# MLP start of a diffusion-backbone kernel: four direct tiles with the last modulation, then seven-product pairs, and the sums of h2 made during the four tiles

## The chip, the core and the metric

The kernel runs on one core of a Trainium2 chip. A core has a matrix engine (PE, 128x128, with its weight loads shown as PEld), a vector engine (DVE), a scalar engine (ACT), GpSimd (POOL) and a sync engine (SP); SP and POOL issue the DMAs. Each engine works through its own queue in order and waits on semaphores. The metric is the device time of one execution in microseconds (us), median of the runs. Before the change it is 1055.24 us (three runs, 1054.97 to 1055.71).

## The reference

One inference step of a layer over 128 context tokens and 512 latent tokens of width 1024. The first sub-layer mixes tokens, the second is a squared-ReLU MLP:

```
mod = silu(c) @ w_ada + b_ada                    # six rows of 1024
h   = layer_norm(x) * (1 + mod[1]) + mod[0]
tm, sf, sb = token_mixer(h, ...)                 # S5 scan, pooling, gates
x   = layer_norm(ALPHA * x + mod[2] * tm) * ln1_g + ln1_b
h2  = layer_norm(x) * (1 + mod[4]) + mod[3]
f   = square(relu(h2 @ w_mlp1 + b_mlp1)) @ w_mlp2 + b_mlp2
x   = layer_norm(ALPHA * x + mod[5] * f) * ln2_g + ln2_b
```

All is float32. The change touches the line of f and the modulation mod[5], the gate of its residual.

## The kernel before

All 640 tokens are handled together, as five token tiles of 128. A float32 operand is split into a high part, rounded to the format that PE reads (a cast on ACT, L321), and the low rest (a subtraction on DVE, L322). A product is three passes: high by high, high by low, low by high. `wsplit` loads one 128x1024 weight block by SP into one of two raw buffers and splits it.

The MLP has 32 hidden tiles of 128 in four quarters of eight. A quarter's first product makes eight tiles f from h2 (`fx`), the second multiplies them with w_mlp2 into two halves of the output, 120 matmuls of 512 columns each, and adds gate times result to x (`add_gated`, L851 and L852). In quarters 2 to 4 two hidden tiles are made together, by seven half-size products in place of eight (`mlp_pair`; Strassen's scheme in Winograd's form). That needs sums of the four blocks of h2 (t1, t2, t4, and t3 in the place of the block b12), made once by `rhs_sums`, and sums of the weights' blocks for each pair (s12, s34, split into w12 and w34; `lhs_pair`). A pair takes 84 matmuls of 320 columns; an ordinary tile 24 of 384 columns and 24 of 256, since h2 is cut after 384 tokens.

The first quarter is different. Its tiles 0 to 4 are made together (`mlp_first`), first for 384 tokens, then for the other 256, so that PE has work while the last token tile of h2 is still in the norm. Tiles 5 to 7 follow one by one (`mlp_in`). Between them stand eight steps of the last modulation (`ada5.step`: four matmuls with a 128x1024 weight loaded by POOL; the class `Ada`, L236), and then `gates`: the finished row gets its bias (L778), is written to DRAM and read back by SP as two tiles with the row in every partition (L783). `rhs_sums` is a generator: one of its eight parts is recorded with each weight of the second product. `residual` (L1045, L1046: x times ALPHA plus bias times gate, for five token tiles) is recorded with the second weight.

A scheduler of the tile framework sets the order on each engine and puts the semaphores; pools with a fixed number of slots decide when a tile can be written: nine slots `x4` (five hold x), eight slots `h` (the out projection's inputs `mx`, later `fx`), three `w10`, two raw weight buffers.

Of the kernel before, what the change touches and what calls it, by code (L numbers as in the profile page):

```python
# [11 lines left out]
F32R = mybir.dt.float32r  # L12
# [5 lines left out]
P = 128  # L18
D = 1024
# [12 lines left out]
SEG_MLP = ((0, 384), (384, 256))  # L32
# [6 lines left out]
def hybrid_kernel(ctx: ExitStack, tc: tile.TileContext, xin, cc, w_ada0, w_ada, w_in, w_glu, w_pa, w_pool, w_pb,  # L39
# [35 lines left out]
    def bank(name="ax"):  # L75
        return pp[0].tile([P, 512], F32, tag="ax", bufs=axn[0], name=nm(name))
# [197 lines left out]
    wa_h = lambda: hslot([P, D], F32, "wa")  # L274
# [49 lines left out]
    def wsplit(src, n=D, to=None):  # L324
        raw = wp.tile([P, D], F32, tag="wr", bufs=2, name=nm("wr"))
        hl = wp.tile([P, 2, D], F32R, tag="wh", name=nm("wh")) if to is None else to
        dma(raw[:, 0:n], src)
        split(raw[:, 0:n], hl[:, 0, 0:n], hl[:, 1, 0:n])
        return hl
# [9 lines left out]
    def mm(hl, xk, segs=SEG):  # L339
        ps = bank2()  # L340
        for k in range(len(xk)):
            mm_k(ps, hl, xk[k], k, len(xk), segs)
        return ps
# [34 lines left out]
    for k in range(KT):  # L378
        pa, pb = bank("pst"), bank("pst")
# [376 lines left out]
    def w8(shape, dtype, name):  # L756
        return xp.tile(shape, dtype, tag="w8", name=nm(name))
# [6 lines left out]
    def brow_tile(src, tile_of, name="brow"):  # L764
        t = tile_of([P, D], name)
        dma(t, src.broadcast_to([P, D]))
        return t
# [6 lines left out]
    def gates(ada, i):  # L774

        row, br = row_tile(), x4([P, 256], "br")
        dma(br, rows[ada.mod].rearrange("(q f) -> q f", q=4).unsqueeze(1).broadcast_to([4, 32, 256]))
        V.tensor_tensor(row, ada.ps[:, 0:256], br, op=ALU.add)  # L778
        dma(grd[i], row)
        gs = []  # L780
        for r in range(2):
            g = xp.tile([P, D], F32, tag="gate", bufs=2, name=nm("gate"))
            dma(g.rearrange("p (q f) -> p q f", q=4),  # L783
                grd[i].rearrange("(q r) f -> r q f", q=4)[r:r + 1].broadcast_to([P, 4, 256]))
            gs.append(g)
        return gs
# [123 lines left out]

    h2k = [h2[:, :, k, :] for k in range(KT)]

    def mlp_in(m):
        ps = mm(wsplit(w_m1[m]), h2k, SEG_MLP)
        return mlp_act(m, [ps[:, n, 0:ln] for n, (_, ln) in enumerate(SEG_MLP)])

    def mlp_act(m, pss):
        fr = x4([P, NT], "fr")
        for (o, ln), ps in zip(SEG_MLP, pss):
            S.activation(fr[:, o:o + ln], ps, AF.Relu, bias=colt[:, C_BM1 + m:C_BM1 + m + 1])  # L920
        V.tensor_tensor(fr, fr, fr, op=ALU.mult)
        f = hslot([P, 2, NT], F32R, "fx")
        split(fr, f[:, 0, :], f[:, 1, :])
        return f

    def mlp_first():

        hls = [wsplit(w_m1[m], to=None if m < 3 else w8([P, 2, D], F32R, "wm")) for m in range(5)]
        pa, pb, pc_ = bank2(), bank2(), bank2()
        x0, x1 = bank("psx"), bank("psx")  # L930
        pss = [[pa[:, 0], pa[:, 1], pb[:, 0], pb[:, 1], pc_[:, 0]],
               [pc_[:, 1], pc_[:, 1, 256:512], x0, x0[:, 256:512], x1]]
        for n, (o, ln) in enumerate(SEG_MLP):
            for hl, ps in zip(hls, pss[n]):
                for k in range(KT):
                    for i, (wh, xh) in enumerate(PASS):
                        T.matmul(ps[:, 0:ln], hl[:, wh, k * P:(k + 1) * P], h2k[k][:, xh, o:o + ln],
                                 start=(k == 0 and i == 0), stop=(k == KT - 1 and i == 2))
        return [mlp_act(m, [pss[n][m][:, 0:ln] for n, (_, ln) in enumerate(SEG_MLP)]) for m in range(5)]

# [3 lines left out]
    def rhs_sums():  # L946
        b11, b12, b21, b22 = [h2[:, :, 4 * i:4 * i + 4, j * HN:(j + 1) * HN] for i in range(2) for j in range(2)]
        t1, t2, t4 = [w10("t").rearrange("p a (k c) -> p a k c", k=4) for _ in range(3)]
        rq.update(b11=b11, b21=b21, b22=b22, t1=t1, t2=t2, t3=b12, t4=t4)

        def whole(b, k):
            f = x4([P, 2, HN], "bf")
            V.tensor_tensor(f, b[:, 0, k:k + 2].bitcast(F32), b[:, 1, k:k + 2].bitcast(F32), op=ALU.add)
            return f

        def put(t, k, f):
            split(f, t[:, 0, k:k + 2], t[:, 1, k:k + 2])

        for k in (0, 2):
            f12, f11 = whole(b12, k), whole(b11, k)  # L960
            V.tensor_tensor(f11, f12, f11, op=ALU.subtract)
            put(t1, k, f11)
            yield
            f22 = whole(b22, k)
            V.tensor_tensor(f12, f22, f12, op=ALU.subtract)
            put(b12, k, f12)
            yield
            V.tensor_tensor(f22, f22, f11, op=ALU.subtract)
            put(t2, k, f22)
            yield  # L970
            f21 = whole(b21, k)
            V.tensor_tensor(f21, f21, f22, op=ALU.subtract)
            put(t4, k, f21)
            yield

    def lhs_pair(m):

# [64 lines left out]
    def residual():  # L1042
        for t in range(NTT):
            tmp = x4([P, D], "tmp")
            V.tensor_tensor(tmp, b2, g5[0 if t else 1], op=ALU.mult)  # L1045
            V.scalar_tensor_tensor(x1s[t], x1s[t], ALPHA, tmp, op0=ALU.mult, op1=ALU.add)  # L1046

    for qf in range(3):
        if qf == 0:
            ada5.load(2)  # L1050
            fx = mlp_first()
            for i, n in ((5, 3), (6, 3), (7, 2)):
                ada5.step(n)
                if i == 7:
                    g5 = gates(ada5, 1)
                    b2 = brow_tile(brow[3:4, :], x4)
                fx.append(mlp_in(i))
        else:
            fx = mlp_in8(qf * 8)
        sums = rhs_sums() if qf == 0 else iter(())  # L1060
        for fh in range(2):
            pa, pb, pc_ = bank2(), bank2(), bank("ps4")
            pt = [pa[:, 0], pa[:, 1], pb[:, 0], pb[:, 1], pc_]
            for kp in range(4):
                hl = wsplit(w_m2[fh, qf * 4 + kp])
                next(sums, None)
                if qf + fh == 0 and kp == 1:
                    residual()
                for kk in range(2):
                    k = 2 * kp + kk  # L1070
                    for t in range(NTT):
                        for i, (wh, xh) in enumerate(PASS):
                            T.matmul(pt[t], fx[k][:, xh, t * P:(t + 1) * P], hl[:, wh, kk * 512:(kk + 1) * 512],  # L1073
                                     start=(k == 0 and i == 0), stop=(k == 7 and i == 2))
            for t in range(NTT):
                add_gated(x1s[t], g5[0 if t else 1], pt[t], fh * 512, fh * 512 + 512)
# [119 lines left out]
```

## Time and profile before

| what | value |
|---|---|
| median of three runs | 1055.24 us |
| profiled execution | 1057.73 us, of which the span is 1056.0 us |
| PE, DVE, ACT, POOL busy | 94%, 65%, 38%, 11% of the span |
| mean granted clock of PE | 0.98 |
| first quarter of the MLP | about 607 to 734 us of the span |

The profile is of one execution. A timeline row gives the start, the length, the engine, the source line, the operation, output<-inputs with their shapes, the count, and in brackets the idle time before it with what ended it. Equal instructions that follow each other are merged into a row. Rows of SP (SPq) and POOL for DMAs show the issue, not the transfer. The granted clock is a share of 2.4 GHz.

### The profile page before, as it was taken

Reading aid. Unit: us, or ns where it says so; the run is one execution under the profiler, and the core shown is the slowest. Engines: PE = TensorE matmul, PEld = TensorE weight load, DVE = VectorE, ACT = ScalarE, POOL = GpSimd, SP = SyncE. Lnnn points to the kernel's source line nnn. Section 1 sums busy time; section 2 is a strip of 40 time slices with the busy share of each in tenths; the row PEclk is TensorE's granted clock in tenths of the full one; section 3 lists DMA queues with packets and bytes.
Section 4 is the critical chain, followed back from the end, with each engine's and each line's share of the span. In section 5 each row is a group of like instructions: output and inputs, shape, how many; then the busy total and the mean of one; then the engine's idle time right before and its main releaser. Section 6 shows DMA issues by size and latency. Waiting matters only on the chain.

```text
span 1056.0 us, 18416 instructions
## 1 busy us (share of the span) xinstructions
PE 991.3 (94%) x7464; PEld 894.4 (85%) x7464; DVE 691.6 (65%) x1203; ACT 403.0 (38%) x683; POOL 110.9 (11%) x164
## 2 busy tenths in 40 slices
PE   4998989998998899999999999989999999999997
PEld 2887878988897799998987898868998899889886
DVE  7698769998921334545847955498864586458686
ACT  5457454322212534422222544313661266116610
POOL 0243210310069000300000000000000000000000
PEclk9999899999999798999999999999999999999999
DMA  9566666855498587977752134513222222212421
GB/s 362 191 176 179 168 182 194 255 166 170 119 284 248 161 253 244 360 231 252 247 182 83 31 110 155 150 45 100 81 100 73 68 80 100 80 60 81 162 78 60
DMA packets 117373, 166.85 MB, mean 158 GB/s; under 512 B 48104, under 2 KB 80872, under 8 KB 117288
## 3 DMA queue, kind: packets, MB, share of 16 engines
q1 hardware_dynamic: 111912, 146.27, 43.9%
q0 software_dynamic: 5376, 19.40, 5.4%
q8 instruction: 59, 0.97, 0.4%
q14 instruction: 26, 0.21, 0.1%
HBM read 135.30 MB, written 30.34 MB: 157 GB/s over the span
## 4 chain that ended last, share of the span: by engine, by line
PE 61%; DVE 16%; DMA 10%; issue 6%; ACT 5%; SPq 2%; DVEq 0%; ACTq 0%; POOL 0%; POOLq 0%
PE ps L336 20%; PE ps L1073 13%; PE ps L1006 8%; PE psx L1006 6%; PE pse L1096 3%; PE ps L886 3%; DVE wh L322 2%; DMA cf<-in_cpk_dram 2%; DMA yd<-y 2%; DVE ta L501 1%; DVE zt L504 1%; PE psa L236 1%; PE psz L480 1%; DVE ta L503 1%; PE ps L1096 1%
## 5 line engine op out<-in xcount | busy, mean ns | idle before, releaser
L336 PE MATMUL ps<-hk,wh 128*128 128x320 f32 x1344 | 217.1, 318 | 10.0 <-DVE sq L542 5.1
L336 PEld LDWEIGHTS ps<-hk,wh 128*128 128x128 f32 x1344 | 202.0, 192 | 18.6 <-issue 6.0
L322 DVE TENSOR_TENSOR wh<-wr,wh 128x1024 fp32r<-128x1024 f32 (+1 forms) x113 | 128.5, 1138 | 101.8 <-ACT wh L321 100.7
L321 ACT CAST wh<-wr 128x1024 fp32r<-128x1024 f32 (+1 forms) x113 | 109.3, 967 | 164.7 <-PE ps L1073 87.6
L1073 PE MATMUL ps<-wh,fx 128*128 128x512 f32 x720 | 166.1, 392 | 5.2 <-DVE x L852 3.0
L1073 PEld LDWEIGHTS ps<-wh,fx 128*128 128x128 f32 x720 | 135.7, 189 | 34.2 <-DVE x L852 3.4
L336 PEld LDWEIGHTS ps<-gx,wh 128*128 128x128 f32 x384 | 56.4, 187 | 3.3 <-issue 2.9
L336 PE MATMUL ps<-gx,wh 128*128 128x320 f32 x384 | 58.7, 310 | 0.0
L336 PEld LDWEIGHTS ps<-vx,wh 128*128 128x128 f32 x384 | 56.4, 188 | 2.5 <-ACT sg L813 2.1
L336 PE MATMUL ps<-vx,wh 128*128 128x320 f32 x384 | 58.1, 311 | 0.0
L224 POOL DMA_DIRECT2D wa<-in_w_ada_dram x32 | 16.9, 534 | 300.8 <-PE psa L236 110.2
L1006 PE MATMUL psx<-h,wh 128*128 128x320 f32 x288 | 47.5, 308 | 0.0
L1006 PE MATMUL ps<-h,w 128*128 128x320 f32 x288 | 46.5, 307 | 0.0
L438 POOL TENSOR_TENSOR cf<-cf 128x64 f32<-128x64 f32 x32 | 24.8, 776 | 191.0 <-DMA cf<-in_cpk_dram 95.7
L1006 PEld LDWEIGHTS psx<-h,wh 128*128 128x128 f32 x288 | 43.7, 187 | 0.2
L1006 PEld LDWEIGHTS ps<-h,w 128*128 128x128 f32 x288 | 43.2, 187 | 0.0
L573 PE MATMUL psy<-zt,q 64*128 64x80 f32 x512 | 42.1, 276 | 0.6 <-issue 0.6
L851 DVE TENSOR_TENSOR ps<-ps,gate 128x512 f32<-128x512 f32 (+2 forms) x39 | 28.1, 749 | 19.2 <-PE ps L1073 14.2
L573 PEld LDWEIGHTS psy<-zt,q 64*128 64x128 f32 x512 | 35.3, 190 | 4.2 <-issue 4.2
L886 PE MATMUL ps<-wo,mx 128*128 128x512 f32 x150 | 36.6, 392 | 0.7 <-ACT wo L321 0.7
L336 PE MATMUL ps<-ybx,wh 128*128 128x320 f32 x192 | 32.6, 328 | 2.7 <-ACT wh L321 2.7
L886 PEld LDWEIGHTS ps<-wo,mx 128*128 128x128 f32 x150 | 27.9, 188 | 7.2 <-ACT wo L321 1.5
(263 smaller groups left out, 1656.9 us busy)
## 6 DMA issues: line engine op xcount, KB each, us to landing
wr<-in_w_m_dram SPq DMA_DIRECT2D x64, 512.0 KB
wa<-in_w_ada_dram POOLq DMA_DIRECT2D x32, 512.0 KB, 5.0
wr<-in_w_in_dram SPq DMA_DIRECT2D x28, 512.0 KB
qd<-q SPq DMA_DIRECT2D x16, 512.0 KB
q<-qd SPq DMA_DIRECT2D x16, 512.0 KB
x<-in_xin_dram SPq DMA_DIRECT2D x10, 512.0 KB
wa<-in_w_ada_dram SPq DMA_DIRECT2D x10, 512.0 KB
tm<-sd SPq DMA_DIRECT2D x8, 512.0 KB
```

Of the source, the lines that this page charges most:

```text
L224: nc.gpsimd.dma_start(w, w_ada[self.mod, :, k * D:(k + 1) * D])
L236: T.matmul(self.ps[32 * q:32 * q + 32, 0:256], sc[:, k, :], w[:, q * 256:(q + 1) * 256], start=(k == 0), stop=(k == KT - 1), skip_group_ch ...
L321: S.copy(hi, raw)
L322: V.tensor_tensor(lo, raw, hi.bitcast(F32), op=ALU.subtract)
L336: T.matmul(ps[:, n, 0:ln], hl[:, wh, k * P:(k + 1) * P], xk[:, xh, o:o + ln], start=(k == 0 and i == 0), stop=(k == nk - 1 and i == 2))
L438: E.tensor_tensor(c[:, :, 3, :], c[:, :, 1, :], c[:, :, 2, :], op=ALU.add)
L573: T.matmul(o, q[d, l, i, :], zt[d, 0:NC // 2, i, 4 * e + l, :], start=(i == 0), stop=False, skip_group_check=True)
L851: V.tensor_tensor(ps, ps, g[:, c0:c1], op=ALU.mult)
L886: T.matmul(ps[:, n, :], mx[k][:, xh, t * P:(t + 1) * P], wo[k][:, wh, n * 512:(n + 1) * 512], start=(k == 0 and i == 0), stop=(k == KT - 1 ...
L1006: T.matmul(ps, hl[:, wh, c + k * P:c + (k + 1) * P], rq[b][:, xh, k, :], start=(start and k == 0 and i == 0), stop=(stop and k == 3 and i ...
L1073: T.matmul(pt[t], fx[k][:, xh, t * P:(t + 1) * P], hl[:, wh, kk * 512:(kk + 1) * 512], start=(k == 0 and i == 0), stop=(k == 7 and i == 2))
L1096: T.matmul(ps[n][:, 0:ln], fx[k][:, xh, t * P:(t + 1) * P], hl[:, wh, o_:o_ + ln], start=(k == 0 and i == 0), stop=(k == 7 and i == 2))
```

## The change

Only four tiles are made by `mlp_first`; tiles 4 to 7 become two pairs. All eight weights of the last modulation are loaded ahead, into `h` slots (`wa_h`), and its eight steps stand in the four tiles' loop, one behind each tile of each part. `rhs_sums` is an ordinary function now, called when the 384-token part is recorded; only the writing of t3, which overwrites a block of h2, is left to the end of the four tiles. `gates` and the residual's bias come before pair 4, `residual` between pair 4 and pair 6.

```
-    def mlp_in(m):
-        ps = mm(wsplit(w_m1[m]), h2k, SEG_MLP)
-        return mlp_act(m, [ps[:, n, 0:ln] for n, (_, ln) in enumerate(SEG_MLP)])
...
-        hls = [wsplit(w_m1[m], to=None if m < 3 else w8([P, 2, D], F32R, "wm")) for m in range(5)]
+        hls = [wsplit(w_m1[m], to=None if m < 3 else w8([P, 2, D], F32R, "wm")) for m in range(4)]
         pa, pb, pc_ = bank2(), bank2(), bank2()
-        x0, x1 = bank("psx"), bank("psx")
-        pss = [[pa[:, 0], pa[:, 1], pb[:, 0], pb[:, 1], pc_[:, 0]],
-               [pc_[:, 1], pc_[:, 1, 256:512], x0, x0[:, 256:512], x1]]
+        pss = [[pa[:, 0], pa[:, 1], pb[:, 0], pb[:, 1]],
+               [pc_[:, 0], pc_[:, 0, 256:512], pc_[:, 1], pc_[:, 1, 256:512]]]
         for n, (o, ln) in enumerate(SEG_MLP):
             for hl, ps in zip(hls, pss[n]):
...
-        return [mlp_act(m, [pss[n][m][:, 0:ln] for n, (_, ln) in enumerate(SEG_MLP)]) for m in range(5)]
+                ada5.step(1)
+            if n == 0:
+                last_sums = rhs_sums()
+        fx = [mlp_act(m, [pss[n][m][:, 0:ln] for n, (_, ln) in enumerate(SEG_MLP)]) for m in range(4)]
+        last_sums()
+        return fx
...
             put(t1, k, f11)
-            yield
             f22 = whole(b22, k)
             V.tensor_tensor(f12, f22, f12, op=ALU.subtract)
-            put(b12, k, f12)
-            yield
+            late.append((k, f12))
...
+        return lambda: [put(b12, k, f) for k, f in late]
...
         if qf == 0:
-            ada5.load(2)
+            ada5.tile_of = wa_h
+            ada5.load(8)
             fx = mlp_first()
-            for i, n in ((5, 3), (6, 3), (7, 2)):
-                ada5.step(n)
-                if i == 7:
-                    g5 = gates(ada5, 1)
-                    b2 = brow_tile(brow[3:4, :], x4)
-                fx.append(mlp_in(i))
+            g5 = gates(ada5, 1)
+            b2 = brow_tile(brow[3:4, :], x4)
+            fx += mlp_pair(4)
+            residual()
+            fx += mlp_pair(6)
...
                 hl = wsplit(w_m2[fh, qf * 4 + kp])
-                next(sums, None)
-                if qf + fh == 0 and kp == 1:
-                    residual()
```

On PE, the end of the direct tiles stood before as follows (psx is the last tiles' sum, psa the modulation's row, ps_7021 tile 5):

```order
L937 MATMUL psx_6724<-h_6177,wm_6711 128x256 x24
L937 MATMUL psx_6725<-h_6177,wm_6716 128x256 x24
L236 MATMUL psa_7001<-wa_6692,sc 32x256 x4
L236 MATMUL psa_7001<-wa_6694,sc 32x256 x4
L336 MATMUL ps_7021<-h_6177,wh_7017 128x384
```

Now pair 4 follows the fourth tile (wh_7042 and w_965, w_966 are its weights, w_965 being w12; the h of wh_7185 is pair 6's, t_6845 and t_6844 are sums of h2):

```order
L933 MATMUL ps_6730<-h_6177,wm_6723 128x256 x24
L236 MATMUL psa_6755<-wa_6706,sc 32x256 x4
L1005 MATMUL psx_7060<-h_6177,wh_7042 128x320 x19
L1005 MATMUL psx_7061<-t_6845,w_965_7049 128x320 x2
L1005 MATMUL ps_7062<-t_6844,w_965_7049 128x320 x2
L1005 MATMUL psx_7061<-t_6845,w_965_7049 128x320 x10
L1005 MATMUL ps_7062<-t_6844,w_965_7049 128x320 x10
L1005 MATMUL ps_7062<-h_6177,w_966_7054 128x320 x12
L1005 MATMUL psx_7060<-h_6177,wh_7042 128x320 x5
L1005 MATMUL psx_7203<-h_6177,wh_7185 128x320 x4
L1005 MATMUL ps_7062<-h_6177,w_966_7054 128x320 x12
```

The three tiles that followed, with the steps between them, are replaced by two pairs, and the second matmul group of pair 4 reads sums of h2 and w12.

On DVE, the first pair's weight sums (s) and w12 stood before in the second product of the first quarter, behind the last sums of h2 (bf, t):

```order
L322 TENSOR_TENSOR t_7249<-bf_7481,t_7249 128x640
L972 TENSOR_TENSOR bf_7559<-bf_7559,bf_7481 128x640
L322 TENSOR_TENSOR wh_7608<-wr_7604,wh_7608 128x1024
L322 TENSOR_TENSOR t_7250<-bf_7559,t_7250 128x640
L987 TENSOR_TENSOR s_1011_7611<-wr_7606 128x512
L991 TENSOR_TENSOR s_1012_7612<-wr_7604,wr_7606 128x512
L988 TENSOR_TENSOR s_1011_7611<-s_1011_7611,wr_7604 128x512
L992 TENSOR_TENSOR s_1012_7612<-wr_7604,s_1011_7611 128x512
L322 TENSOR_TENSOR w_1013_7615<-s_1011_7611,w_1013_7615 128x1024
```

Now they stand behind the sums, the activations of the four tiles (fr, fx) and the modulation's row:

```order
L917 TENSOR_TENSOR fr_7009<-fr_7009 128x640
L917 TENSOR_TENSOR fr_7016<-fr_7016 128x640
L322 TENSOR_TENSOR fx_7006<-fr_7002,fx_7006 128x640
L322 TENSOR_TENSOR fx_7013<-fr_7009,fx_7013 128x640
L322 TENSOR_TENSOR fx_7020<-fr_7016,fx_7020 128x640
L778 TENSOR_TENSOR row_7027<-psa_6755,br_7028 128x256
L986 TENSOR_TENSOR s_963_7045<-wr_7040 128x512
L990 TENSOR_TENSOR s_964_7046<-wr_7038,wr_7040 128x512
L987 TENSOR_TENSOR s_963_7045<-s_963_7045,wr_7038 128x512
L991 TENSOR_TENSOR s_964_7046<-wr_7038,s_963_7045 128x512
L322 TENSOR_TENSOR w_965_7049<-s_963_7045,w_965_7049 128x1024
L322 TENSOR_TENSOR w_966_7054<-s_964_7046,w_966_7054 128x1024
```

From the last token tile's first split to w_965 DVE now has 32 operations of 128x640.

On DVE, the residual (tmp, x) stood before among the second product's weights and evacuations:

```order
L322 TENSOR_TENSOR wh_7382<-wr_7381,wh_7382 128x1024
L322 TENSOR_TENSOR h_6177<-bf_7251,h_6177 128x2x320
L1045 TENSOR_TENSOR tmp_7298<-brow_7177,gate_7175 128x1024
L1045 TENSOR_TENSOR tmp_7301<-brow_7177,gate_7173 128x1024
L1046 SCALAR_TENSOR_TENSOR x_777_5598<-x_777_5598,tmp_7298 128x1024
```

Now it stands among pair 4's additions (L1016 to L1028) and in front of pair 6's sums; the additions free the sums that pair 4's last products go into:

```order
L322 TENSOR_TENSOR wh_7185<-wr_7181,wh_7185 128x1024
L1016 TENSOR_TENSOR fr_7064<-psx_7061,fr_7064 128x320
L1019 TENSOR_TENSOR fr_7064<-ps_7062,fr_7064 128x320
L1020 TENSOR_TENSOR fr_7064<-ps_7062,fr_7064 128x320
L1044 TENSOR_TENSOR tmp_7166<-brow_7036,gate_7034 128x1024
L322 TENSOR_TENSOR wh_7200<-wr_7183,wh_7200 128x512
L1045 SCALAR_TENSOR_TENSOR x_777_5598<-x_777_5598,tmp_7166 128x1024
L1025 TENSOR_TENSOR fr_7063<-ps_7062,fr_7064 128x320
L1044 TENSOR_TENSOR tmp_7169<-brow_7036,gate_7032 128x1024
L1045 SCALAR_TENSOR_TENSOR x_778_5600<-x_778_5600,tmp_7169 128x1024
L1028 TENSOR_TENSOR fr_7064<-ps_7062,fr_7064 128x320
```

The first use of a gate is now in front of L1025 and of everything of pair 6 but its first weight.

## Rows read from the trace of the kernel before

**Rows 1.** The page: engines' busy time, share of the span, instructions.
```profile
PE 991.3 (94%) x7464; PEld 894.4 (85%) x7464; DVE 691.6 (65%) x1203; ACT 403.0 (38%) x683; POOL 110.9 (11%) x164
```
**Rows 2.** Stages: length, busy PE, PEld, DVE, ACT, POOL (instructions), clock, DMA, GB/s.
```profile
645.80:672.00 26.20, 25.85 (x196) 22.14 (x193) 9.12 (x11) 6.10 (x10) 3.14 (x6) 1.00 0.56 190
672.00:700.00 28.00, 27.92 (x124) 22.81 (x122) 20.46 (x21) 7.72 (x10) 0.00 (x0) 1.00 0.30 76
700.00:708.00 8.00, 2.83 (x12) 2.03 (x12) 8.00 (x13) 1.78 (x2) 0.00 (x0) 0.97 0.18 66
734.00:784.00 50.00, 50.00 (x337) 49.18 (x336) 39.35 (x58) 28.49 (x42) 0.00 (x0) 1.00 0.22 76
```
**Rows 3.** Waits of PE, 590 to 740: total us, times, longest.
```profile
PE ps L1073 <- DVE wh L322: 2.2, 1, 2.2
```
**Rows 4.** Timeline of PE, first quarter of the MLP.
```profile
607.09 5.02 PE L937 MATMUL ps<-h,wh 128*128 128x384 f32 x28
...
639.07 5.81 PE L937 MATMUL psx<-h,wm 128*128 128x256 f32 x48
...
657.95 0.64 PE L236 MATMUL psa<-wa,sc 128*32 128x256 f32 x8
...
672.10 27.82 PE L1073 MATMUL ps<-wh,fx 128*128 128x512 f32 x122
...
707.96 25.91 PE L1073 MATMUL ps<-wh,fx 128*128 128x512 f32 x107 [3.00 <-DVE x L852]
```
**Rows 5.** Timeline, end of the out projection and last token tile's norm.
```profile
600.29 6.96 PE L886 MATMUL ps<-wo,mx 128*128 128x512 f32 x30
...
606.29 1.05 ACT L321 CAST wh<-wr 128x1024 fp32r<-128x1024 f32 x1 [4.47 <-DMA wr<-in_w_m_dram]
...
619.84 1.21 DVE L322 TENSOR_TENSOR wm<-wr,wm 128x1024 fp32r<-128x1024 f32 x1
...
625.82 0.69 DVE L322 TENSOR_TENSOR h<-h2f,h 128x512 fp32r<-128x512 f32 x1 [3.21 <-ACT h L321]
```
**Rows 6.** DMA, 432 to 456: queue's share of 16 engines; issues, KB, us to landing.
```profile
q0 software_dynamic: 2086, 7.56, 79.9%
...
wa<-in_w_ada_dram POOLq DMA_DIRECT2D x9, 512.0 KB, 11.0
```
**Rows 7.** The page: DMA issues of the whole span, KB, median us to landing.
```profile
wa<-in_w_ada_dram POOLq DMA_DIRECT2D x32, 512.0 KB, 5.0
```
**Rows 8.** DVE by line and shape, 600 to 760: busy us, mean ns.
```profile
L322 DVE TENSOR_TENSOR wh<-wr,wh 128x1024 fp32r<-128x1024 f32 x17 | 20.7, 1218 | 7.4 <-ACT wh L321 7.2
...
L953 DVE TENSOR_TENSOR bf<-h 128x640 f32<-128x640 f32 x8 | 6.5, 822 | 0.0
...
L1045 DVE TENSOR_TENSOR tmp<-brow,gate 128x1024 f32<-128x1024 f32 x5 | 5.9, 1220 | 5.9 <-issue 5.9
...
L987 DVE TENSOR_TENSOR s<-wr 128x512 f32<-128x512 f32 x3 | 2.0, 683 | 0.0
```
**Rows 9.** Timeline of DVE, two sums' operations one behind the other.
```profile
716.15 0.83 DVE L953 TENSOR_TENSOR bf<-h 128x640 f32<-128x640 f32 x1
...
716.89 0.83 DVE L968 TENSOR_TENSOR bf<-bf,bf 128x640 f32<-128x640 f32 x1
```
**Rows 10.** Timeline, from the modulation's row to the first use of a gate.
```profile
670.22 0.33 SPq L779 DMA_DIRECT2D grd<-row  x1
...
672.53 0.93 SPq L783 DMA_DIRECT2D gate<-grd  x2
...
688.06 2.36 DVE L1045 TENSOR_TENSOR tmp<-brow,gate 128x1024 f32<-128x1024 f32 x2 [5.91 <-issue]
...
689.31 1.06 ACT L321 CAST wh<-wr 128x1024 fp32r<-128x1024 f32 x1 [7.89 <-DMA wr<-in_w_m_dram]
```
**Rows 11.** Timeline of PE, restart after a wait.
```profile
346.73 0.90 PE L336 MATMUL ps<-ph,wh 128*128 128x320 f32 x2 [7.87 <-ACT ph L321]
```
**Rows 12.** Stage behind that restart, columns as in rows 2.
```profile
346.70:355.00 8.30, 8.27 (x37) 7.32 (x38) 3.06 (x6) 2.47 (x4) 0.00 (x0) 0.50 0.27 93
```

More of the change, by code (lines that the diff above doesn't have):

```diff
@@ L957, in put @@
             split(f, t[:, 0, k:k + 2], t[:, 1, k:k + 2])
+        late = []
         for k in (0, 2):
@@ L962, in rhs_sums @@
             put(t1, k, f11)
-            yield
             f22 = whole(b22, k)
             V.tensor_tensor(f12, f22, f12, op=ALU.subtract)
-            put(b12, k, f12)
-            yield
+            late.append((k, f12))
             V.tensor_tensor(f22, f22, f11, op=ALU.subtract)
             put(t2, k, f22)
-            yield
             f21 = whole(b21, k)
@@ L973, in rhs_sums @@
             put(t4, k, f21)
-            yield
+        return lambda: [put(b12, k, f) for k, f in late]
     def lhs_pair(m):
@@ L1049, in hybrid_kernel @@
         if qf == 0:
-            ada5.load(2)
+            ada5.tile_of = wa_h
+            ada5.load(8)
             fx = mlp_first()
-            for i, n in ((5, 3), (6, 3), (7, 2)):
-                ada5.step(n)
-                if i == 7:
-                    g5 = gates(ada5, 1)
-                    b2 = brow_tile(brow[3:4, :], x4)
-                fx.append(mlp_in(i))
+            g5 = gates(ada5, 1)
[3 more added lines that the diff above has]
+            fx += mlp_pair(6)
         else:
             fx = mlp_in8(qf * 8)
-        sums = rhs_sums() if qf == 0 else iter(())
         for fh in range(2):
```

## Prediction

> **What bounds the kernel now.** I read the page first: the matrix engine (PE) is busy for 94% of the span [rows 1], so time is lost only where PE waits or runs on a slow clock. The change lies in the first quarter of the MLP, so I next read the stages of that quarter, one by one. While tiles 5 to 7 run (645.8 to 672.0) the vector engine (DVE) has 9 us of work in 26; in the first half of the second product it has 20 in 28, and between 700 and 708 it is busy all the time while PE does 2.8 us of work [rows 2]. The reader is to see that DVE is idle beside the first product and crowded beside the second. The waits of PE in this quarter are short: 2.2 us for a weight's low half that stands behind other DVE work, and 3.0 us for the sums into x [rows 3, 4]. So before the change at most some 5 us of waiting can be won here, and the quarter ends, for this argument, where the last matmul of its second product ends: 707.96 + 25.91 = 733.9 us [rows 4].
>
> **What goes on PE.** From the starts and lengths of runs of equal matmuls, one with 384 columns takes 5.02/28 = 0.179 us, with 256 columns 5.81/48 = 0.121; the second product's take 27.82/122 = 0.228 [rows 4]. The second quarter's four pairs, 336 matmuls with 320 columns, fill 734 to 784: 50/337 = 0.148 [rows 2]. Four direct tiles cost 4 x 24 x (0.179 + 0.121) = 28.8 us; two pairs cost 2 x 84 x 0.148 = 24.9. PE saves 3.9 us of work. The eight modulation steps stay eight, 0.6 us each (0.64 by the row, less the overlap with the next) [rows 4]. Their loads now go into the slots of the out projection's inputs, each as soon as the last token tile has read it, so they are in place before PE wants them; the wait they had cost is a few tenths.
>
> **The start of the vector chain.** The last token tile's matmuls, 0.232 us each (6.96/30), end at 607.25 [rows 5]; each six of them free one slot, 1.4 us, so the eight loads of 512 KB are issued between 597 and 607, beside the third and fourth MLP weight's. Before, the third weight's cast began at 606.29 after a wait of 4.47 for its load [rows 5]. How much that load is slowed isn't shown. From 432 to 456, among nine such loads that filled 79.9% of the engines, they took 11.0 us to land [rows 6] where 5.0 is the usual [rows 7]: 2.2 times as long. Bounds: 0, and 1.2 times the wait, 5.4. I take 2.2 us, nearer to 0, since the eight come spread over ten microseconds. ACT holds the norm's square root behind that cast, and the last token tile's norm hangs on it, so PE, too, is 2.2 late. The Trainium skill, page "DMA: Bandwidth & Descriptors", section "Queues, rings and completion order", says that each DMA engine takes turns between queue rows packet by packet. By that rule a weight's load beside the eight keeps half of each engine and is late by no more than it takes alone, 4.5 us: as an estimate, by the rule the sum below would be at most 30.8, by the row's 2.2 times at most 31.7. No row of before shows which of the two holds.
>
> The first half of the last token tile's split started at 625.82 and takes 0.69; the split of a fifth weight in front of it, 1.2 us, is gone [rows 5]. So DVE can begin the sums at 626.5 - 1.2 + 2.2 = 627.5.
>
> **The sums before the first pair.** By the order, between that point and the low half of w12, which the first pair's second multiplication needs, DVE now has 32 operations of 128x640 (the sums, their splits, the squares and splits of the four tiles), seven of 512 columns or about as long, and two of 1024. A 128x640 one takes 0.82 us [rows 8]; two that don't depend on each other start 0.74 apart [rows 9], one that waits for the one before it comes a few hundredths after its end, so 0.80 is the mean: 25.6 us. Seven at 0.68 are 4.8, two at 1.22 are 2.4 [rows 8]. In all 32.8: w12 is there at 660.3. The modulation's row, which starts the gates, stands four short operations and w12 earlier: 660.3 - 1.2 - 4 x 0.68 - 0.4 for w12's cast = about 656.
>
> PE meanwhile ends the four tiles where it ended five before (639.07 + 5.81 = 644.9 [rows 4]), less one tile (24 x 0.300 = 7.2), plus eight steps (4.8), plus the 2.2 above: 644.7. Before w12 it can do 22 matmuls of the pair, 3.3 us (and even these wait in part for a copy that takes the slot of the row's bias). **PE idles 660.3 - 644.7 - 3.3 = 12.3 us**, where before it worked through.
>
> **The gates.** From the issue of the row's write to the first use of a gate took 670.22 to 688.06, 17.8 us, in which DVE stood for 5.9 [rows 10]. In the new order that first use, the residual, stands in DVE's queue in front of the additions of pair 4 and in front of all sums of pair 6. So DVE stops there until 656 + 17.8 = 673.8. Next in its queue is the split of a weight loaded behind the gates: before, such a load was there 1.25 us after the gates (689.31 against 688.06) [rows 10]; with the cast's 0.6 and the split's 0.7 that is 676.4. One residual operation (1.2) and the addition (0.5) follow: 678.1. PE has 61 matmuls to do from 660.3, 9.0 us, and the last of pair 4 waits for that addition: idle from about 669.3 (673 at half clock) to 678.1.
>
> From there to pair 6's w12 DVE has eight residual operations of 1.22 (9.8), one addition (0.5), two splits of 0.82, four sums of 0.68 and w12 itself (1.2): 15.8, so 693.9. PE has 19 matmuls for that time (2.8 us) and idles about another 12 us. Then pair 6 needs 65 matmuls, 9.6 us, and the second product, 240 x 0.228 = 54.7, with nothing of the sums or the residual in its way; its two waits of before are gone.
>
> **The clock.** After a wait of 7.87 us PE restarted at 346.73 and the granted clock was 0.50 from 346.7 to 355.0, the lower level of 1.2 GHz [rows 11, 12]: 4.2 us lost. Three such gaps come here. What the first two lose lies within the next wait; the third's 4.2 lies on the path.
>
> **The sum.** 693.9 + 9.6 + 54.7 + 4.2 = 762.4, against 733.9: 28.5 us more. Quarters 2 to 4 keep their order, so it stays to the end. Round it to 28: DVE's starts overlap a little. The profiled execution took 1057.73 us (span 1056.0 and 1.73 around it), 2.5 above the median 1055.24; it would become 1085.7, the median **1083 us**.
>
> Ends of the unknown costs: the loads 0 to 5.4 (-2.2, +3.2); the spacing of DVE's operations 0.74 to 0.86 (0.82 and a few hundredths) (-1.9, +1.9); the clock, nothing or a second 4.2 (-4.2, +4.2); the gates, as quick as the usual 5.0 us of a 512 KB load after 2.3 us for the row's write [rows 7, 10], 10.5 less, or another 512 KB in front of them, about 3 more. All low: 1064; all high: 1095 or 1096.
>
> **Rivals.**
> 1. *Quick gates.* The gates' 17.8 us may come in part from the weight loaded after them [rows 10]. If they land in 7.3, DVE is not stopped, and pair 6's w12 comes 10.5 earlier: 28 - 10.5 = 17.5, 1073 us. For it: 512 KB usually land in 5.0 [rows 7]. Against: the gates are read in small pieces, and the same loads stand around them again. Chance 0.20.
> 2. *Only the first pair waits.* If the residual were passed by, only the 12.3 us and one cold start (4.2) would be added, and the 3.9 of work and 5.2 of waits saved: +7.4, 1063. The order speaks against it: DVE takes the residual first. Chance 0.06.
> 3. *Faster: the sums fit beside the tiles.* DVE is nearly idle there before [rows 2]. If the sums hid, PE would save 3.9 of work and 5.2 of waits: 1046. This decides if w12 is ready when PE comes for it, at 644.7 + 3.3 = 648.0, that is if the 32 operations took 0.42 us in place of 0.80. The measured 0.82 [rows 8] excludes that as far as a row can. Chance 0.04.
> 4. *The loads weigh more.* If the eight loads hold up the third and fourth weight by their full 5.4 and the gates, too, come late, 28 + 3.2 + 3: 1089. Chance 0.08.
> 5. *The change doesn't do what it says*, the sums being finished beside the second product as before and only the pairs counting: 1055.2 - 3.9 = 1051 at best. The order places all of them ahead of the first pair's w12. Chance 0.01.
>
> The forecast has 0.61. A change of 0.2%, 2.1 us, is about the least that a measurement tells here from none. Faster: 0.04 + 0.01, same 0.02 (from rival 2's edge), slower 0.93. The range for 8 in 10 leaves out rivals 2, 3 and 5 and the far ends: 1067 to 1092.
>
> **What would show it.** Right: in the profile after, two or three gaps of PE between about 645 and 695, ended by the low half of w12, by L1025 and by pair 6's w12; DVE without a gap from about 627 to 660 and then one at the residual's first operation, until the gates land; no PE wait in the second product; its end near 762. Wrong: the first gap shorter than 8 us (the chain is shorter than counted), a residual that starts before 668 (quick gates), or PE at full clock after the gaps. The prediction falls altogether if PE enters pair 4 without a wait.

## The result, and the profile after

The changed kernel takes **1084.9 us** (median of 4 runs, 1082.6 to 1086.7) against 1055.5 beside it: ratio **1.0273** [1.0247, 1.0298], 2.7% slower. The profiled span grew from 1056.0 to 1083.4, the mean granted clock fell from 0.980 to 0.961. The forecast was 1083.

On the page PE is now busy for 92% of the span, with 24 instructions fewer and 6.4 us more of busy time than in [rows 1]. Of the 6.4, 4.1 lie in the stretch of the first quarter defined below (120.5 before, 124.6 now): there the matmuls saved are outweighed by matmuls at the lower clock.

```profile
PE 997.7 (92%) x7440; PEld 900.3 (83%) x7440; DVE 702.2 (65%) x1221; ACT 409.9 (38%) x691; POOL 110.2 (10%) x164
```

The waits of PE between 590 and 775 (total us, times, longest). The two waits of the second product [rows 3, 4] are gone; five others, 27.3 us in all, stand ahead of it.

```profile
PE psx L1005 <- ACT fr L1014: 15.7, 2, 8.2
PE pst L902 <- DVE tmp L896: 5.1, 1, 5.1
PE ps L1005 <- DVE fr L1025: 4.9, 1, 4.9
PE psx L1005 <- ACT w L321: 1.7, 1, 1.7
```

The timeline of PE shows where they are; each matmul group behind a wait is slow (12 of 320 columns take 3.57 us where 12 without a wait take 1.92). The second product itself runs without a break, as in [rows 4] it did not.

```profile
608.39 5.02 PE L933 MATMUL ps<-h,wh 128*128 128x384 f32 x28
618.47 1.97 PE L902 MATMUL pst<-ident,tmp 128*128 128x128 f32 x8 [5.06 <-DVE tmp L896]
620.09 8.93 PE L933 MATMUL ps<-h,wh 128*128 128x384 f32 x44
...
650.58 2.03 PE L1005 MATMUL psx<-h,wh 128*128 128x320 f32 x12
660.06 2.23 PE L1005 MATMUL psx<-h,wh 128*128 128x320 f32 x7 [7.45 <-ACT fr L1014]
...
679.19 3.57 PE L1005 MATMUL ps<-t,wh 128*128 128x320 f32 x12 [4.86 <-DVE fr L1025]
690.99 1.17 PE L1005 MATMUL psx<-h,wh 128*128 128x320 f32 x3 [8.23 <-ACT fr L1014]
...
707.62 53.04 PE L1068 MATMUL ps<-wh,fx 128*128 128x512 f32 x233
```

To compare kernels whose earlier parts start a microsecond apart I use one **stretch**: from the start of the four (or five) tiles' first matmuls (the row with x28) to the first matmul of the next quarter. Before it is 733.71 - 607.09 = 126.6 us, now 760.49 - 608.39 = 152.1: **25.5 us** of the 27.4 by which the span grew. Of the rest, 1.3 lie ahead of it (608.39 against 607.09) and 0.6 behind.

What the waits are made of, from the timelines of ACT, DVE and SP:

```profile
611.58 1.05 ACT L321 CAST wh<-wr 128x1024 fp32r<-128x1024 f32 x1 [8.46 <-DMA wr<-in_w_m_dram]
615.13 1.04 ACT L321 CAST wm<-wr 128x1024 fp32r<-128x1024 f32 x1 [2.50 <-DMA wr<-in_w_m_dram]
616.08 0.29 ACT L859 ACTIVATE rs<-mv,epst 128x1 f32<-128x1 f32 x1
...
659.59 0.43 ACT L1014 COPY fr<-psx 128x320 f32<-128x320 f32 x1 [1.86 <-DVE row L778]
...
690.51 0.43 ACT L1014 COPY fr<-psx 128x320 f32<-128x320 f32 x1 [4.84 <-DVE tmp L1044]
...
632.96 1.56 DVE L954 TENSOR_TENSOR bf<-h 128x640 f32<-128x640 f32 x2
...
659.09 0.42 DVE L778 TENSOR_TENSOR row<-psa,br 128x256 f32<-128x256 f32 x1
662.42 2.36 DVE L322 TENSOR_TENSOR w<-s,w 128x1024 fp32r<-128x1024 f32 x2 [0.38 <-ACT w L321]
...
659.53 0.33 SPq L779 DMA_DIRECT2D grd<-row  x1
661.72 0.93 SPq L783 DMA_DIRECT2D gate<-grd  x2
...
675.04 1.22 DVE L1044 TENSOR_TENSOR tmp<-brow,gate 128x1024 f32<-128x1024 f32 x1 [3.97 <-DMA gate<-grd]
678.65 0.48 DVE L1025 TENSOR_TENSOR fr<-ps,fr 128x320 f32<-128x320 f32 x1
...
693.89 2.42 DVE L322 TENSOR_TENSOR w<-s,w 128x1024 fp32r<-128x1024 f32 x2
```

Read against [rows 5]: the third weight's cast comes 3.2 us behind the first MLP matmul, before 0.8 ahead of it; the fourth's comes 6.7 behind it, before 1.8. The norm's root (L859) stands on ACT behind that fourth cast, as it did before the change, so it comes 4.9 us later. In the timeline of ACT of the kernel before:

```profile
608.90 1.05 ACT L321 CAST wm<-wr 128x1024 fp32r<-128x1024 f32 x1 [1.56 <-DMA wr<-in_w_m_dram]
609.86 0.29 ACT L859 ACTIVATE rs<-mv,epst 128x1 f32<-128x1 f32 x1
```

PE's waits of 7.45 and 8.23 us end with ACT's copy L1014, which reads the sum that PE then goes on adding to. The first copy stands until the modulation's row is made (L778), the second until the last multiplication of the residual (L1044); w12 is used 2.4 and 2.9 us behind the ends of these waits. Against [rows 10]: from the row's write to the gates' first use 15.5 us in place of 17.8, but now with PE waiting behind it.

The stages (columns as in rows 2) show the price of the waits in clock: 0.50 behind the waits that end at 660.06, 679.19 and 690.99, and 1.00 in the second product.

```profile
660.00:665.00 5.00, 4.79 (x16) 4.17 (x17) 4.36 (x6) 2.73 (x4) 0.00 (x0) 0.50 0.64 198
680.00:685.00 5.00, 2.76 (x11) 2.35 (x9) 3.70 (x5) 2.84 (x5) 0.00 (x0) 0.50 0.00 0
...
690.00:695.00 5.00, 2.27 (x7) 1.80 (x7) 5.00 (x7) 2.46 (x3) 0.00 (x0) 0.50 0.10 25
710.00:760.00 50.00, 50.00 (x222) 41.39 (x221) 21.24 (x27) 9.95 (x11) 0.00 (x0) 1.00 0.26 85
```

### The profile page after: what moved, and what is told of

It reads as the page before. It is cut to its first block, busy times and chain, and to the rows that moved or that the text cites. A ratio compares the mean times of both kernels' runs of the same rounds, so it can differ in the third digit from the quotient of the medians.

```text
span 1083.4 us, 18397 instructions
## 1 busy us (share of the span) xinstructions
PE 997.7 (92%) x7440; PEld 900.3 (83%) x7440; DVE 702.2 (65%) x1221; ACT 409.9 (38%) x691; POOL 110.2 (10%) x164
## 4 chain that ended last, share of the span: by engine, by line
PE 66%; DVE 16%; DMA 9%; ACT 4%; issue 3%; SPq 1%; DVEq 0%; ACTq 0%; POOL 0%
PE ps L336 20%; PE ps L1068 15%; PE ps L1005 9%; PE psx L1005 6%; PE ps L886 3%; PE pse L1091 3%; DMA wr<-in_w_m_dram 3%; DVE wh L322 2%; PE psy L573 2%; DMA cf<-in_cpk_dram 2%; DVE ta L501 2%; DVE zt L504 2%; DVE ta L503 1%; PE psz L480 1%; PE psa L236 1%
## 5 line engine op out<-in xcount | busy, mean ns | idle before, releaser
L336 PE MATMUL ps<-hk,wh 128*128 128x320 f32 x1344 | 221.3, 322 | 11.6 <-DVE sq L542 6.5
L336 PEld LDWEIGHTS ps<-hk,wh 128*128 128x128 f32 x1344 | 206.0, 195 | 20.1 <-issue 7.5
L1005 PE MATMUL psx<-h,wh 128*128 128x320 f32 x336 | 57.3, 314 | 15.7 <-ACT fr L1014 15.7
L1005 PEld LDWEIGHTS psx<-h,wh 128*128 128x128 f32 x336 | 52.0, 191 | 17.0 <-ACT fr L1014 16.3
L1005 PE MATMUL ps<-h,w 128*128 128x320 f32 x336 | 54.3, 308 | 0.0
L1005 PEld LDWEIGHTS ps<-h,w 128*128 128x128 f32 x336 | 50.3, 187 | 0.1
L851 DVE TENSOR_TENSOR ps<-ps,gate 128x512 f32<-128x512 f32 (+2 forms) x39 | 28.1, 749 | 22.4 <-PE ps L1068 17.4
```

The source lines that it names most:

```text
L336: T.matmul(ps[:, n, 0:ln], hl[:, wh, k * P:(k + 1) * P], xk[:, xh, o:o + ln], start=(k == 0 and i == 0), stop=(k == nk - 1 and i == 2))
L851: V.tensor_tensor(ps, ps, g[:, c0:c1], op=ALU.mult)
L1005: T.matmul(ps, hl[:, wh, c + k * P:c + (k + 1) * P], rq[b][:, xh, k, :], start=(start and k == 0 and i == 0), stop=(stop and k == 3 and i ...
```

## The experiments

Ten kernels ran. All ratios are to the kernel before, run beside them.

| run | stretch, us | median, us | ratio, interval |
|---|---|---|---|
| before | 126.6 | 1055.5 | 1 |
| changed | 152.1 | 1084.9 | 1.0273 [1.0247, 1.0298] |
| e1_loads_behind | 148.0 | 1079.1 | 1.0189 [1.0169, 1.0209] |
| e2_residual_after | 140.4 | 1074.1 | 1.0144 [1.0122, 1.0167] |
| e3_no_sums | 151.0 | 1082.4 | 1.0224 [1.0202, 1.0246] |
| e4_four_direct | 124.5 | 1057.1 | 0.9980 [0.9963, 0.9998] |
| e5_hoist | 147.7 | 1082.6 | 1.0237 [1.0204, 1.0270] |
| e6_hoist_no_sums | 142.8 | 1076.7 | 1.0177 [1.0146, 1.0208] |
| e7_best | 129.2 | 1062.5 | 1.0052 [1.0026, 1.0078] |
| e8_four_behind | 119.5 | 1050.9 | 0.9926 [0.9898, 0.9954] |
| e9_all_three | 124.5 | 1058.4 | 1.0005 [0.9978, 1.0032] |
| e10_gates_later | 123.3 | 1057.2 | 0.9989 [0.9963, 1.0015] |

Medians of different batches don't compare: the kernel before took 1057 to 1059 beside e1 to e10. And e3's profiled span (1083.8) is the changed kernel's (1083.4) though its ratio is 0.5% lower; so steps of some microseconds are read from the stretch, the verdict on a kernel from its ratio. The stretch is read from one execution of each kernel. In the six that load the modulation's weights as the changed kernel does (the changed one, e2 to e6), PE's wait at the transposes alone lies between 4.4 and 5.4 us, so a difference of 1 us says little.

**e1, the loads.** `ada5.queue = dma`, and `ada5.load(8)` from the line ahead of `mlp_first()` to behind its four `wsplit`s.

> The changed kernel, with the last modulation's eight loads of 512 KB issued by SyncE behind the four MLP weights, in place of GpSimd's queue ahead of them. My theory: in the changed kernel the eight loads delay the third MLP weight (its cast began at 611.58 after a wait of 8.46 us, against 606.29 and 4.47 before the change), so the last token tile's split and every later step are late by some 4 us. Without them in front, that cast comes at about 607, the sums begin about 4 us earlier and the whole is 1080 to 1082 us, with the three waits of the pairs still there. Rival: the loads are hidden and the time lies only in the vector engine's order; then 1085 and the same rows.

The stretch is 4.1 us shorter, as expected; the waits of the pairs stayed (15.7 in two, 6.0, 1.7). The ratio fell by 0.8%, some 9 us and so by more than the stretch; that part is not explained. The mechanism is not quite the one I named: by the order four of the eight loads still stand ahead of the third weight, and its cast is still 1.8 us behind the first MLP matmul. But the fourth weight's cast comes 4.0 us behind that matmul in place of 6.7, and the norm's root now stands on ACT ahead of it, so that the transposes wait for 1.1 us in place of 5.1. How much each of the two gave is not separated.

**e2, the residual.**

```diff
             fx += mlp_pair(4)
-            residual()
             fx += mlp_pair(6)
+            residual()
```

> The changed kernel, with the residual behind both pairs in place of between them. My theory: the residual waits for the gates (first use at 675.04) and holds L1025's addition and the sums of pair 6 behind it in the vector engine's queue, and its bias tile holds a slot that pair 6's copy wants. With it behind, the waits of 4.9 and 8.2 us and the third restart at half clock go; pair 6's own weights still come behind the gates (cast at 676.26), so pair 6 ends near 691 in place of 707, the residual's ten operations (12 us) then stand in front of the second product's weights for 2 to 4 us: 1071 to 1075 us. Rival 1, the sums ahead of the first pair set everything: 1083 to 1086. Rival 2, the residual behind costs in the second product as much as it saves (a wait of over 8 us there): 1083 or more.

11.7 us less in the stretch, 1074.1: the size was met, and both rivals are out. The wait of 8.2 and the 1.7 behind it are gone, but the 4.9 at L1025 stayed (5.5 here): what holds it in this kernel is not the residual but pair 6's second weight, which SP issues behind the gates (662.09 against 661.07).

```profile
PE psx L1005 <- ACT fr L1014: 7.4, 1, 7.4
PE ps L1005 <- DVE fr L1025: 5.5, 1, 5.5
PE pst L902 <- DVE tmp L896: 5.0, 1, 5.0
```

```profile
676.33 0.69 DVE L986 TENSOR_TENSOR s<-wr 128x512 f32<-128x512 f32 x1 [5.83 <-DMA wr<-in_w_m_dram]
```

**e3, the sums.** In `rhs_sums` all from `t1, t2, t4 = ...` on is replaced:

```diff
+        rq.update(b11=b11, b21=b21, b22=b22, t1=b11, t2=b21, t3=b12, t4=b22)
+        return lambda: None
```

> The changed kernel without the sums of h2: the pairs of this quarter and the later ones read blocks of h2 itself, so the output is not the reference's; matmuls, weights and copies are as many. My theory: the 24 operations (0.8 us each, 19 us) ahead of the first pair's low half of w12 are gone, so the first wait of 7.5 us goes and the row of the modulation comes right after its last step (651 in place of 659); the gates still need some 15.5 us after it, so the first use is near 667 and the wait for it stays, in the vector engine and then in the tensor engine: about 8 us less, 1075 to 1079. Rival, the sums are all of the loss: 19 us or more less, 1066 or below. Rival, the gates land by another clock than the row's (a queue full of other loads): first use still at 675 and the time within 2 us of 1085.

My theory fell: 1.1 us in the stretch in place of 8, and the gates' first use at 674.90. Without the sums DVE idles, and yet the row comes at 658.43. The timeline of e3 says why:

```profile
653.54 2.28 DVE L322 TENSOR_TENSOR fx<-fr,fx 128x640 fp32r<-128x640 f32 x3
654.38 0.62 SPq L777 DMA_DIRECT2D br<-in_rows_dram  x1
658.43 0.42 DVE L778 TENSOR_TENSOR row<-psa,br 128x256 f32<-128x256 f32 x1 [1.27 <-DMA br<-in_rows_dram]
...
660.16 1.17 PE L982 MATMUL psx<-h,wh 128*128 128x320 f32 x3 [6.85 <-ACT fr L991]
```

The row's bias goes into one of the nine x4 slots, and its turn is the slot of the first tile's `fr`, which is free only when that tile is split, behind PE's last step; its load then takes 4 us. The squares and splits of all four tiles (eight operations, here seven of them ahead of the row) stand ahead of the row and of w12 in DVE's queue besides. So a **second cover**, that is a second cause that hides behind the first, lies under the sums and ends less than 2 us ahead of them: the row comes 48.9 us after the stretch's start here, 50.7 in the changed kernel.

**e5 and e6, both covers.** The row's bias is loaded ahead into the row's own tile, and the row, the gates and pair 4's weight sums are recorded ahead of the squares; e6 leaves out the sums as well.

```diff
+            br5 = bias_row(ada5, lambda *a: row_tile())
...
+        lhs = lhs_pair(4)
+        g5 = gates(ada5, 1, br5)
         fx = [mlp_act(m, [pss[n][m]...
...
-            fx += mlp_pair(4)
+            fx += mlp_pair(4, lhs)
```

> The changed kernel, with the row's bias loaded ahead into the row's own tile (so that it needs no slot that the four tiles hold), and pair 4's weight sums and the gates recorded ahead of the four tiles' squares. It follows the run without sums, in which the tensor engine's first wait stayed at 6.9 us and the row at 658.4, because the row's bias waited for a slot of the first tile and the four tiles' squares and splits stood ahead of w12. My theory now: two covers, within 1 us of each other, hold w12 and the row: the sums, and the four tiles' own eight operations with their slots. Taking the second alone brings both some 6 us nearer: the row at about 653, w12 near 657 (first wait 3 to 4 us in place of 7.5), the gates' first use near 669 in place of 675, the whole 5 to 7 us shorter than the changed kernel: 1078 to 1080, ratio 1.020 to 1.023. Rival, the sums alone set the row and w12 whatever is recorded where: no gain, 1085.

> The same with the sums of h2 left out (the pairs read blocks of h2 itself, so the output is not the reference's). My theory: with both covers gone w12 is ready before the tensor engine asks, its first wait vanishes, the row comes right behind the last modulation step (651 to 652) and the gates' first use near 667; L1025 still waits behind it (5 to 8 us) and pair 6 for the residual. 7 to 10 us shorter than the changed kernel: 1075 to 1078, and 1.5 to 4 us shorter than the version with the sums. Rival, a third thing holds the first pair: the first wait stays at 6 us or more.

With sums, the first wait is 3.1 and 0.8 in place of 7.45 (timeline of PE, e5), and the stretch 4.4 us shorter; 5 to 7 were expected. The row came 4.9 us earlier, the residual only 3.7, because the tile `b2`, issued behind the gates, was then the last to land. Pair 6's weights are now issued ahead of the gates (649.95 and 652.18 on SP, the gates at 654.07), and yet PE waits for 4.6 us at pair 4's additions, since the residual's first operation stands ahead of them on DVE.

```profile
652.59 0.71 PE L1012 MATMUL psx<-t,w 128*128 128x320 f32 x2 [3.11 <-ACT w L321]
654.08 3.03 PE L1012 MATMUL psx<-t,w 128*128 128x320 f32 x10 [0.79 <-DVE w L322]
...
668.27 1.22 DVE L1051 TENSOR_TENSOR tmp<-brow,gate 128x1024 f32<-128x1024 f32 x1 [5.29 <-DMA brow<-in_brow_dram]
```

Without sums too (e6) the first wait is gone altogether and the stretch is 9.3 us shorter, as expected; the waits at L1009 (7.0) and for the residual (8.2) remain.

```profile
654.11 1.92 PE L989 MATMUL psx<-h,w 128*128 128x320 f32 x12
...
671.80 3.39 PE L989 MATMUL ps<-h,wh 128*128 128x320 f32 x12 [6.96 <-DVE fr L1009]
```

Taken together: leaving the sums out is worth 1.1 us while the other cover stands and 4.9 when it is gone (1.0 of the 4.9 is the wait at the transposes, 5.4 in e5 and 4.4 in e6); lifting the other cover is worth 4.4 with the sums in and 8.2 without them.

**e4 and e8, without pairs.** Tiles 4 to 7 one by one, sums and residual beside the second product as before the change; e8 has e1's loads as well. Against the changed kernel:

```diff
-            fx += mlp_pair(4)
-            residual()
-            fx += mlp_pair(6)
+            fx += [mlp_in(i) for i in range(4, 8)]
```

> The changed kernel's first part (four tiles, the last modulation's eight loads early and its steps inside them), with tiles 4 to 7 one by one as before the change, the sums made beside the second product and the residual at its second weight, as before. My theory: no wait of the tensor engine between the products, since 28.8 us of direct tiles cover the gates; only the eight loads' delay of the third weight (4 to 5 us) is left, less about 2 to 3 us of waits in the second product that the earlier gates spare: 1056 to 1060. Rival 1, the early modulation costs nothing: 1052 to 1054. Rival 2, the early loads and steps are themselves a large part of the loss: 1065 or more.

> The version with four direct tiles 4 to 7, and the eight loads by SyncE behind the weights in place of GpSimd's queue ahead of them. My theory: the early loads' delay of the third weight (a wait of 4.9 us at the transposes) is all that this version loses against an undisturbed start, so the second product ends 3 to 4 us earlier (near 731), ratio to the kernel before 0.993 to 0.996. Rival: the delay is made good later under the direct tiles, or comes from the transfers' volume and not from their order: 0.998 as before.

e4: no wait but that of the transposes (4.9), 1057.1, ratio 0.998; the stretch is 2.1 us shorter than before the change. The loads' delay is in it, and the second product's two waits (5.2 us) are gone. So beginning with four tiles and the modulation costs nothing on balance, and the whole loss lies in the pairs, with the sums that they need ahead of them and the residual between them. e8 takes another 5.0 us and **beats both kernels**: 0.9926, a little under what was expected. Its timelines (ACT, then PE): the root ahead of the fourth cast, transposes almost without a wait, then no gap to the end of the second product.

```profile
609.68 1.05 ACT L322 CAST wh<-wr 128x1024 fp32r<-128x1024 f32 x1 [6.85 <-DMA wr<-in_w_m_dram]
610.63 0.29 ACT L860 ACTIVATE rs<-mv,epst 128x1 f32<-128x1 f32 x1
612.09 1.05 ACT L322 CAST wm<-wr 128x1024 fp32r<-128x1024 f32 x1 [1.17 <-DMA wr<-in_w_m_dram]
...
613.96 1.09 PE L903 MATMUL pst<-ident,tmp 128*128 128x128 f32 x8 [0.83 <-DVE tmp L897]
...
644.87 28.43 PE L337 MATMUL ps<-h,wh 128*128 128x384 f32 x192
673.15 54.57 PE L1075 MATMUL ps<-wh,fx 128*128 128x512 f32 x240
```

**e7, one pair.** Tiles 4 and 5 direct, `lhs = lhs_pair(6)`, then the gates' reads, then pair 6; loads as in e1, the row ahead of the squares as in e5, the residual in three pieces, and two of the sums of h2 in the tiles of the gates.

> A version meant to beat both: the four tiles with the modulation and the sums of the change, tiles 4 and 5 one by one (14 us of tensor engine under which the sums end), only pair 6 with seven products; the eight loads by SyncE behind the weights; the row recorded ahead of the squares and the gates read behind pair 6's weights; the residual in three pieces at the second, third and fourth weight of the second product. My theory: the tensor engine waits nowhere over 2 us, saves 2 us of work by the one pair and up to 5 us of the waits before, and pays some 1 to 4 us for the early loads: its second product ends near 730 in place of 733.9, ratio to the kernel before 0.993 to 0.998. Rival: pair 6's w12, behind the last sums and the splits of tiles 4 and 5 in the vector engine's queue, comes 4 us late or more, and the ratio is 1.000 or above.

It did not beat the kernel before (1.0052). The rival's w12 was 1.8 us late, not 4; the larger wait, 4.8, came from a place that I had not seen: the second product's first weight lands behind the gates, and DVE's split of it stands ahead of pair 6's additions. In part this is the version's own doing: by SP's waits the gates' reads stood for 8.9 us until the two sums in their tiles were split, and were issued at 655.70, 10.1 us behind the row's write (645.57), where the changed kernel took 2.2.

```profile
674.42 1.22 DVE L323 TENSOR_TENSOR wh<-wr,wh 128x1024 fp32r<-128x1024 f32 x1 [8.91 <-ACT wh L322]
...
676.67 0.49 DVE L1036 TENSOR_TENSOR fr<-ps,fr 128x320 f32<-128x320 f32 x1
...
677.22 3.57 PE L1021 MATMUL ps<-h,w 128*128 128x320 f32 x12 [4.77 <-DVE fr L1036]
```

**e9 and e10, the pairs kept.** e9 is e1, e2 and e5 in one kernel; e10 reads the gates behind pair 6's weights (its edit against e9):

```diff
-            b2 = brow_tile(brow[3:4, :], x4)
             fx += mlp_pair(4, lhs)
+            lhs = lhs_pair(6)
+            g5 = gates_read(1)
+            b2 = brow_tile(brow[3:4, :], x4)
-            fx += mlp_pair(6)
+            fx += mlp_pair(6, lhs)
             residual()
```

> The changed kernel with three of the edits at once, both pairs kept: the eight loads by SyncE behind the weights (alone: 4.1 us less between the four tiles' first matmul and the second product's last), the residual behind pair 6 (alone 11.7 less), the row and pair 4's weight sums ahead of the four tiles' squares (alone 4.4 less). My theory: they act at different places of one chain, so they add up: that stretch takes about 132 us in place of 152.1 (before the change 126.6), the ratio to the kernel before is 1.006 to 1.011; the wait that stays is that for pair 6's weight behind the gates' transfers. Rival: they cover one another, and less than 15 us goes: 137 us or more, ratio 1.013 or above.

> The same, with the reads of the gates behind pair 6's two weights on SyncE's queue in place of ahead of them. My theory: the wait at L1025 that the run with the residual behind still had (5.5 us, its vector engine standing 5.8 us for a weight) is the weight's place behind the gates' 1 MB, so it goes here, and with it a restart at half clock: 4 to 7 us less than the kernel with the three edits, the stretch at 125 to 128 us, ratio 1.001 to 1.006; the residual then starts later, beside the second product, without holding the tensor engine more than 3 us. Rival: the weight is late for another reason (its own slot, the volume of the transfers around it): the same wait of 4 us or more. Second rival: the wait only moves to the second product's first weight, which now stands behind the gates: a wait of 4 us or more there and no gain.

e9 came out better than expected (132 us, ratio 1.006 or more): its stretch is 124.5, 27.6 us less than the changed kernel's; the three edits alone make 20.2. They do more than add up, and again it is two covers. With the weight sums earlier, pair 4's raw weights are freed earlier, and by SP's timeline both of pair 6's loads (647.81, 650.05) are issued ahead of the gates (651.88), as in e5. So the wait at pair 4's additions, which e2 kept because of that weight and e5 because of the residual, is gone with both. It was the wait that e10 was to remove; its loads and gates stand in e9's order on SP (646.78, 649.02, gates 650.89), and it adds only 1.2 us. Waits of PE at the pairs, in e9 and then in e10:

```profile
PE psx L1014 <- ACT w L322: 3.1, 1, 3.1
PE ps L1014 <- ACT w L322: 1.6, 1, 1.6
...
PE psx L1014 <- DVE w L323: 1.2, 2, 0.9
```

```profile
PE psx L1017 <- ACT w L322: 3.1, 1, 3.1
...
PE psx L1017 <- DVE w L323: 1.2, 2, 0.9
```

So the change's loss is undone with all its pairs in place, but they win nothing over the kernel before that the ratio shows (0.9989, its interval holds 1; the stretch is 3.3 us shorter): the first pair still waits 4.0 us behind the sums, and the matmuls behind the wait are slow. PE is busy for about 27.1 us with the four tiles in e10 and for 28.3 in e8, so that little over 1 us of the 3.9 is left. Direct tiles (e8) remain ahead.

## Why the prediction was right

Its mechanism held: PE waits ahead of each pair, DVE works without a gap to the row and then stands for the gates with L1025 and pair 6 behind it. e2 (11.7 us for the residual's place) and e4 (no loss without pairs) show it. But that the time came out within 2 us of the forecast is in part luck: several terms were off in opposite directions. In the stretch the sum has 28.5 us and 25.5 were measured; 1.3 us ahead of it and 0.6 behind it, which the sum doesn't have, bring the span to 27.4.

- **The loads, 2.2 us.** Mis-sized, inside the bounds 0 to 5.4: PE waits 5.06 us at the transposes, before 0, and then loses 1.9 to the clock (1.97 - 1.09 and 8.93 - 7.87). e1 gives 4.1 of it back, e8 against e4 5.0. The step named the third weight alone; the root stood behind the fourth's cast, before the change too. From its issue on SP to its cast the third weight took 3.6 us before (602.65 to 606.29) and 7.6 now (603.95 to 611.58), the fourth 3.9 before (605.05 to 608.90) and 8.8 now (606.35 to 615.13): 4.0 and 4.9 us more. The prediction drew a bound from the rule of turns between queue rows (the Trainium skill, "DMA: Bandwidth & Descriptors", "Queues, rings and completion order"): a load is late by no more than it takes alone. Its 4.5 us for that were ACT's wait and not the load's time; with 3.6 and 3.9 in their place both loads exceed the bound, and what takes the rest is not shown.
- **The sums' start, 627.5.** It was 632.96: 1.3 by the earlier part, the rest by the loads and the slow clock after them. The fifth weight's split, taken off at 1.2 us, saved 0.5 (9.9 us from L896 to L896 on DVE in place of 10.4).
- **The chain of 32.8 us.** 632.96 to the end of w12's split, near 663.6, is 30.6: the spacing was 0.74 for most operations, the lower of the two ends. That the sums hold the row and w12 is only half the reason: e3 and e6 show a second cover of nearly the same length, which the prediction had counted into the chain (the four tiles' eight operations) or passed over (the bias's slot).
- **First wait, 12.3 us.** 7.45. "Shorter than 8 us" was named as a sign against it; PE came 6 us later than 644.7, w12 only 3, and at half clock PE took longer for what it had to do meanwhile. The wait also ended otherwise than named: with the copy into the slot of the row's bias, which the prediction has only in brackets, and not with w12.
- **The gates, 17.8 us.** 15.5, first use at 675.04 against 673.8. The quick gates (rival 1) did not come.
- **L1025 at 678.1**: its end was 679.1 (678.65 and 0.48). The reason named second, a weight behind the gates, is by e2 sufficient alone; e5 and e6 show that the residual is so too.
- **Pair 6's w12 at 693.9**: its split begins at 693.89 and ends near 695.1. PE's third wait is not the 12 us for w12, but 8.23 for the copy behind the residual and then 1.74 for w12's cast.
- **The clock, 4.2 us.** On the path behind pair 6's w12 it was 1.3: from 695.1 to 760.66 PE took 65.6 us for what the sum puts at 9.6 + 54.7 = 64.3. Over the whole stretch it was more, but there, the prediction argued, the next wait hides it: waits of 27.3 us (5.06 + 7.45 + 4.86 + 8.23 + 1.74), less 3.9 of work and 6.0 of waits before (2.2, 3.0, and two of 0.4 and 0.3 at other lines), leave 25.5 - 17.4 = 8.1 us for the clock and what these terms don't show. PE's busy time says the same: it rose by 4.1 us while 3.9 us of work went.
- **The end of the second product at 762.4**: 760.66, without a wait in it.

Of the other rivals, faster sums (3) and a lone first wait (2) were excluded as argued, and the sums stand ahead of w12 on DVE, as the order said (against 5). Rival 4 came half true: the loads held the third and fourth weight up by 4.0 and 4.9 us of its 5.4, but the gates were not late.

## What to carry to other kernels

When an experiment takes one cause away and nothing moves, look for a second cover that ends at the same time: take away both, each alone and together, before a cause is named. A wait on a transfer costs what stands behind the waiting instruction in its engine's queue, and every load issued behind that transfer. Work that is moved under an engine's cover must leave room for the first consumer: 3.9 us of saved matmuls did not pay for 4.0 us of waiting behind the sums that they need and the slow matmuls after it.

## What the runs showed of the hardware

The transfers around the gates are slow for their volume. From 655 to 680 the changed kernel moved 2.89 MB, most packets under 2 KB, at 116 GB/s, and the transfers took 48% of the engines' time; the nine loads of [rows 6] moved 7.56 MB in 24 us, 315 GB/s, in 79.9%. By the time that the engines were busy that is about 240 GB/s against 394.

```profile
DMA packets 1765, 2.89 MB, mean 116 GB/s; under 512 B 100, under 2 KB 1380, under 8 KB 1764
```

A load of 128 KB (the row's bias in e3) was used 4.05 us after its issue, little less than the usual 5.0 of 512 KB [rows 7].

Waits of 3.1 and 0.9 us, two matmuls apart, already cost clock: in e10 the ten matmuls behind them take 3.01 us, where twelve take 1.92 without a wait; the granted clock from 649.4 to 654.0 was 0.63.
